# Decoder trunk: weights packed by the host into contiguous groups, x and p also passed transposed, and the first FFN chunk computed with weights stationary

## The chip, the cores and the metric

The kernel runs on one core of one Trainium2 chip. The metric is the device time of one execution in microseconds, the median over runs; lower is better. All inputs and the output are float32 in HBM. Whatever the host does to the inputs before the launch is not in the time.

## The reference, cut to what matters

```python
# x: (1, 256, 1024); p: (2, 1, 256, 256); DEPTH = 2, D_FF = 2816
def swiglu(x, w_in, w_out):
    h = x @ w_in                       # w_in: 1024 x 5632
    gate, up = h[..., :D_FF], h[..., D_FF:]
    return (silu(gate) * up) @ w_out   # w_out: 2816 x 1024

for i in range(DEPTH):
    if i == 1: k_nope, k_rope, v = shared_kv(x, ...)
    x = layer_norm(ALPHA * x + 0.5 * swiglu(x, ffn1_w_in[i], ffn1_w_out[i]))
    x = layer_norm(ALPHA * x + (fox_mixer(x) if i == 0 else mla_mixer(x)))
    x = layer_norm(ALPHA * x + 0.5 * swiglu(x, ffn2_w_in[i], ffn2_w_out[i]))
    gate = sigmoid(x @ ple_w_gate[i] + ple_b_gate[i])
    x = layer_norm(ALPHA * x + gate * (p[i] @ ple_w_proj[i]))
```

There are 256 tokens, two layers and four SwiGLU FFNs. The first layer mixes with forgetting attention (FoX), the second with multi-head latent attention (MLA).

## The kernel before, in words

**Precision.** Every operand of a matmul is split into a high part (rounded by an ACT copy into the float32r type) and a low part (source minus high part, by DVE). One product is three matmuls: high x high, high x low, low x high. The splits of weights are the lines `L194` (ACT) and `L195` (DVE) in the profile; the splits of activations are the helper `parts` (`L522` ACT, `L523` DVE). Nearly all matmuls are issued by the helper `mm`, line `L513`, and all transposes by `transpose`, `L517` (a matmul against the identity `ident`).

**Weights.** A class `Stream` owns the weights. A trial pass records in which order the program uses weight units; the real pass then loads groups of up to 128 x 2048 floats (1 MB) in that order into a ring of `NRAW = 3` raw buffers (`raw`). All loads are DMAs on SP's queue, and a raw buffer is loaded again once both of its units are split. Each unit (128 x 1024) is split into a slot: ten slots `hl`, and four tiles that are lent as slots while nobody else needs them (`ota`, `otb`, `qk`, `fs`). When a unit is split is decided while the program is built, from modelled times of PE, ACT, DVE and DMA; on the chip the order of each engine's instructions is then fixed. A weight in HBM lies as the reference has it, so a `w_in` group is read as two DMAs of 256-column strips, rows of 1 KB, and a `w_out` group as one DMA with rows of 4 KB.

**An FFN.** `ffn` walks over eleven chunks `c` of 256 gate and 256 up columns. `HT(c)` keeps a block of 128 weight columns stationary and streams the 256 tokens of the transposed activations `xT` (256 columns per matmul, 96 matmuls), so the hidden values come out transposed, as the second matmul needs them: SiLU and product (`L707`, `L708`), then `parts`. Chunks alternate between two rings of two PSUM banks, `h` and `tr`. `W(c)` multiplies with `w_out` into four `y` banks (512 columns per matmul). A chunk may be given a "turn", some transposes put between its first and second unit: `T(c)` transposes the hidden values of a chunk that came out with tokens on partitions, `ple_transpose` those of `p`, and `spare` transposes the identity.

**The very first chunk.** `first` computes chunk 0 of the first FFN (`cold=True`) while data still arrive. In `setup`, x is loaded in eight 128 x 256 pieces that alternate on SP's queue with pieces of the first weight groups, and two matmuls on the zeroed `mask` (`spin`, `L493`; the profile has two records for each) keep TensorE at work. `first` transposes x piece by piece (`turn`), spins twice more, and multiplies with x stationary and 512 weight columns moving (`part`, 48 matmuls), one 128-row slice `k` at a time, the two token tiles staggered. The hidden values have tokens on partitions and get SiLU and product per token tile (`act`, `L675`, `L676`); chunk 1 then carries the turn `T(0, "h")`. In all, sixteen transposes of x and four of chunk 0 run in this stage.

**The per-layer input p.** In the second FFN of each layer, `ple_load` loads p at chunk 6 and `ple_transpose` (four transposes and `parts`) is the turn of chunk 8.

**The rest.** FoX and MLA are orders written out by hand; LayerNorm is `ln` (its first read of x is `L574`, its scale and shift are loaded into `gb` by `load_gb`).

Of the kernel before, what the change touches and what calls it, by code (L numbers as in the profile page):

```python
# [31 lines left out]
FINE = 4  # L32
# [59 lines left out]
class Recorder:  # L92
# [10 lines left out]
    lend = reclaim = check = load = busy = pair = split = ahead = later = split_now = fill = pump  # L103
# [3 lines left out]
class Stream:  # L107
# [66 lines left out]
    def split(self, between=lambda: None, half=False):  # L174
# [18 lines left out]
        def part(c):  # L193
            nc.scalar.activation(hi[:, c], src[:, c], AF.Copy)  # L194
            nc.vector.tensor_tensor(lo[:, c], src[:, c], hi[:, c].bitcast(F32), op=ALU.subtract)  # L195

        if self.ready < FINE:
            self.hl[key] = w
            part(slice(0, 1))
            between()  # L200
            part(slice(1, 2))
        elif key[0] == "pb":
            nc.gpsimd.memset(w[:, 0, :].bitcast(F32), 0.0)
            lo = w[32:33, 0, :n]
            part(slice(None))
        elif half:
            nc.scalar.activation(hi, src, AF.Copy)
            self.busy(act=n)

            def rest():  # L210
                nc.vector.tensor_tensor(lo, src, hi.bitcast(F32), op=ALU.subtract)
                self.busy(dve=n)
                self.split_done(key, w)

            self.rest = rest
            return
        else:
            part(slice(None))
# [113 lines left out]
def make_loads(a):  # L332
    def rows(ap, k0, n):
        return ap[k0 * 128 : (k0 + n) * 128, :].rearrange("(k p) c -> p k c", p=128)

    def loads(q, g, raw, fine, between):
        k, i = g[0], g[-1]
        if k == "win":
            w = a[g[2]][0][g[1]]
            c = g[3]  # L340
            r = raw.rearrange("p (k c) -> p k c", c=512)
            n = fine
            for k0 in range(0, 4, n):
                if n == 1 and (i, k0) in between:
                    between[i, k0]()
                for s in range(2):
                    c0 = DFF * s + 256 * c
                    q.dma_start(
                        r[:, k0 : k0 + n, 256 * s : 256 * s + 256], rows(w[:, c0 : c0 + 256], 4 * i + k0, n)
                    )  # L350
        elif k == "fv":
            w = a["fox_w_in"][0]
            q.dma_start(raw.rearrange("p (k c) -> p k c", c=512), rows(w[:, 2048:2560], 4 * i, 4))
        elif k == "fvb":
            w = a["fox_w_in"][0]
            q.dma_start(raw.rearrange("p (k c) -> p k c", c=256), rows(w[:, 2560:2816], 0, 8))
        elif k == "fvc":
            w = a["fox_w_in"][0]
            n = 6 - 4 * i
            q.dma_start(raw[:, 0 : 272 * n].rearrange("p (k c) -> p k c", c=272), rows(w[:, 2816:3088], 6 * i, n))  # L360
        elif k in ("fk", "fq"):
            w = a["fox_w_in"][0]
            c = (1024 if k == "fk" else 0) + 256 * i
            q.dma_start(raw.rearrange("p (k c) -> p k c", c=256), rows(w[:, c : c + 256], 0, 8))
        elif k in ("wout", "fo", "pg", "pp", "mo"):
            if k == "wout":
                w = a[g[2]][1][g[1]]
            elif k == "fo":
                w = a["fox_w_o"][0]
            elif k == "mo":  # L370
                w = a["mla_w_o"][0]
            elif k == "pg":
                w = a["ple_w_gate"][g[1]]
            else:
                w = a["ple_w_proj"][g[1]]
            q.dma_start(raw.rearrange("p (k c) -> p k c", c=1024), rows(w, 2 * i, 2))
        elif k == "pb":
            q.dma_start(raw[0:1, 0:1024], a["ple_b_gate"][g[1] : g[1] + 1, :])
        elif k == "kd":
            q.dma_start(raw[:, 0:1280].rearrange("p (k c) -> p k c", c=320), rows(a["kv_w_down"], 4 * i, 4))  # L380
        elif k == "dq":
            q.dma_start(raw[:, 0:1536].rearrange("p (k c) -> p k c", c=384), rows(a["mla_w_dq"][0], 4 * i, 4))
        elif k == "qr":
            w = a["mla_w_uq"][0]
            for s in range(2):
                kk = 2 * i + s
                if kk < 3:
                    q.dma_start(
                        raw[:, 1024 * s : 1024 * s + 1024].rearrange("p (h d) -> p h d", d=64),
                        w[128 * kk : 128 * kk + 128, :, 128:192],  # L390
                    )
        elif k == "kvv":
            w = a["kv_w_up"]
            for kk in range(2):
                q.dma_start(
                    raw[:, 512 * kk : 512 * kk + 512].rearrange("p (h d) -> p h d", d=128),
                    w[128 * kk : 128 * kk + 128, 4 * i : 4 * i + 4, 128:256],
                )
        elif k == "kq":
            for kk in range(5):  # L400
                w, r = (a["kv_w_up"], kk) if kk < 2 else (a["mla_w_uq"][0], kk - 2)
                q.dma_start(
                    raw[:, 256 * kk : 256 * kk + 256].rearrange("p (h d) -> p h d", d=128),
                    w[128 * r : 128 * r + 128, 2 * i : 2 * i + 2, 0:128],
                )
        else:
            raise KeyError(g)
# [15 lines left out]
class Trunk:  # L423
# [33 lines left out]
    def setup(self):  # L457
# [29 lines left out]
        self.S.lend("ota", "otb", "qk", "fs")  # L487
# [12 lines left out]
    def load_x(self, t, q):  # L500
        c = slice(256 * q, 256 * q + 256)
        self.dma(self.x[t][:, c], None if self.rec else self.a["x"][0, 128 * t : 128 * t + 128, c])


# [100 lines left out]
    def ffn(self, li, which, lni, kv=False, ple=False, at=None, cold=False):  # L605
# [12 lines left out]
        def first():  # L618

            ps = [self.bank("h") for _ in range(2)]  # L620

            def part(t, k, w):
                for i, j in SWEEPS[4][0]:
                    self.mm(
                        ps[t], self.xT[:, t, i, k, :], w[:, j, 512 * (k % 2) : 512 * (k % 2) + 512],
                        k == 0 and (i, j) == (0, 0), k == 7 and (i, j) == SWEEPS[4][0][-1],
                    )

            def turn(t, q):
                tr = self.bank("tr")  # L630
                c = slice(2 * q, 2 * q + 2)
                for i in range(2):
                    k = 2 * q + i
                    self.transpose(tr[:, 128 * i : 128 * i + 128], self.x[t][:, 128 * k : 128 * k + 128])
                self.parts(
                    self.xT[:, t, 0, c, :], self.xT[:, t, 1, c, :],
                    tr[:, 0:256].rearrange("p (k c) -> p k c", c=128),
                )

            S.hold = True  # L640
            turn(0, 0)
            self.spin(2)
            old = None
            for u in range(4):
                key = ("win", li, which, 0, u)

                def mid():
                    turn(1, u)
                    if u:
                        part(1, 2 * u - 1, old)  # L650
                    part(0, 2 * u, S.hl.get(key, Dummy()))

                S.split(mid)
                if self.rec:
                    mid()
                w = old = self.use(key)
                if u < 3:
                    turn(0, u + 1)
                else:
                    S.split()  # L660
                part(0, 2 * u + 1, w)
                if u == 3:
                    act(0, 0, ps[0])
                    S.split()
                part(1, 2 * u, w)
            S.split()
            part(1, 7, w)
            S.hold = False
            act(0, 1, ps[1])
# [21 lines left out]
        def HT(c, what=None):  # L691
            ring = "tr" if c % 2 == cold else "h"
            ps = [self.bank(ring) for _ in range(2)]
            for u in range(4):
                if u == 1 + (cold and c == 1) and what:
                    what()
                w = self.use(("win", li, which, c, u))
                for kk, b in ((kk, b) for kk in range(2) for b in range(4)):
# [6 lines left out]
                    )  # L705
            gt = self.tl([128, 768], F32, "P", 2)[:, 0:512]
# [35 lines left out]
        def spare(ring):  # L742
# [33 lines left out]
    def ple_load(self, li):  # L776
        self.ple_p = self.tl([128, 512], F32, "g4", 5)
        for t in range(2):
            self.dma(
                self.ple_p[:, 256 * t : 256 * t + 256],  # L780
                None if self.rec else self.a["p"][li, 0, 128 * t : 128 * t + 128, :],
            )

    def ple_transpose(self):
        nc = self.nc
        pt = self.ple_p
        tr = self.bank("h")
# [831 lines left out]
```

## Time and profile before

| what | us |
|---|---|
| median of 3 runs | 1083.85 (1083.05 to 1084.26) |
| profiled execution, first to last instruction (span) | 1080.8 |
| what lies around the span, against the median | 3.05 |
| PE busy | 1065.8 |
| PE weight loads busy | 971.2 |
| DVE busy | 718.8 |
| ACT busy | 543.3 |

No time of its own is recorded for the profiled execution beside its span, so the span is set against the median of the runs. The busy time of an engine is the time in which it has an instruction in flight; matmuls are pipelined, so PE's busy time contains short gaps. In the chain that ended last each piece is followed back from the end of the program to what released it. The DMA queue moved 197.43 MB, at a mean of 184 GB/s over the span with the instruction loads.

### The profile page before, as it was taken

Reading aid. Unit: us, or ns where it says so; the run is one execution under the profiler, and the core shown is the slowest. Engines: PE = TensorE matmul, PEld = TensorE weight load, DVE = VectorE, ACT = ScalarE, POOL = GpSimd, SP = SyncE. Lnnn points to the kernel's source line nnn. Section 1 sums busy time; section 2 is a strip of 40 time slices with the busy share of each in tenths; the row PEclk is TensorE's granted clock in tenths of the full one; section 3 lists DMA queues with packets and bytes.
Section 4 is the critical chain, followed back from the end, with each engine's and each line's share of the span. In section 5 each row is a group of like instructions: output and inputs, shape, how many; then the busy total and the mean of one; then the engine's idle time right before and its main releaser. Section 6 shows DMA issues by size and latency. Waiting matters only on the chain.

```text
span 1080.8 us, 17731 instructions
## 1 busy us (share of the span) xinstructions
PE 1065.8 (99%) x7210; PEld 971.2 (90%) x7210; DVE 718.8 (67%) x1042; ACT 543.3 (50%) x806; POOL 73.2 (7%) x104
## 2 busy tenths in 40 slices
PE   9999999999999999999999999999999999999996
PEld 7989999899879999998899999988899889898986
DVE  4665645888797545558966564388777886455566
ACT  4565433666646444444555443336576465444431
POOL 0000000222200000000320000012200000000000
PEclk9999999999999999999999999999999999999999
DMA  8787752653358756455588564343445568565502
GB/s 270 230 312 241 245 181 83 195 166 137 114 172 290 254 181 190 148 201 156 164 275 266 185 194 165 89 105 112 140 145 169 174 225 308 191 206 192 182 13 78
DMA packets 151428, 198.54 MB, mean 184 GB/s; under 512 B 11954, under 2 KB 130994, under 8 KB 151348
## 3 DMA queue, kind: packets, MB, share of 16 engines
q1 hardware_dynamic: 151348, 197.43, 55.8%
q8 instruction: 56, 0.92, 0.3%
q14 instruction: 24, 0.20, 0.1%
HBM read 196.35 MB, written 1.05 MB: 183 GB/s over the span
## 4 chain that ended last, share of the span: by engine, by line
PE 90%; DVE 6%; issue 2%; ACT 2%; POOL 1%; DVEq 0%; POOLq 0%; ACTq 0%
PE y L513 32%; PE h L513 32%; PE tr L513 23%; PE tr L517 2%; DVE hl L195 2%; DVE x L593 1%; ACT hl L194 1%; DVE st L575 0%; DVE x L574 0%; PE h L517 0%; DVE PT L523 0%; ACT P L1460 0%; PE tr L1100 0%; DVE g L833 0%; POOL rs L585 0%
## 5 line engine op out<-in xcount | busy, mean ns | idle before, releaser
L195 DVE TENSOR_TENSOR hl<-raw,hl 128x1024 fp32r<-128x1024 f32 (+3 forms) x276 | 321.4, 1183 | 152.0 <-ACT hl L194 150.4
L194 ACT ACTIVATE hl<-raw 128x1024 fp32r<-128x1024 f32 (+3 forms) x276 | 274.4, 1016 | 187.0 <-PE y L513 95.0
L513 PE MATMUL y<-hl,g 128*128 128x512 f32 x816 | 190.7, 390 | 0.0
L513 PEld LDWEIGHTS y<-hl,g 128*128 128x128 f32 x816 | 152.0, 188 | 30.7
L513 PE MATMUL tr<-xT,hl 128*128 128x256 f32 x1512 | 177.3, 277 | 0.0
L513 PEld LDWEIGHTS tr<-xT,hl 128*128 128x128 f32 x1512 | 174.6, 188 | 0.9 <-DVE hl L195 0.2
L513 PE MATMUL h<-xT,hl 128*128 128x256 f32 x1464 | 174.0, 278 | 0.1
L513 PEld LDWEIGHTS h<-xT,hl 128*128 128x128 f32 x1464 | 170.0, 188 | 1.5 <-DVE qk L523 0.3
L513 PE MATMUL h<-hl,xT 128*128 128x512 f32 (+2 forms) x348 | 80.9, 379 | 0.5 <-DVE xT L523 0.4
L513 PEld LDWEIGHTS h<-hl,xT 128*128 128x128 f32 x348 | 61.5, 188 | 13.0 <-DVE xT L523 0.9
L513 PE MATMUL y<-hl,xT 128*128 128x512 f32 (+3 forms) x360 | 65.4, 334 | 0.0
L513 PEld LDWEIGHTS y<-hl,xT 128*128 128x128 f32 x360 | 55.5, 188 | 6.3 <-ACT xT L522 0.4
L585 POOL TENSOR_TENSOR rs<-ve,mhalf 128x1 f32<-128x1 f32 x16 | 15.2, 952 | 601.2 <-DVE ve L584 601.2
L522 ACT ACTIVATE xT<-tr 128x512 fp32r<-128x512 f32 (+1 forms) x36 | 19.2, 550 | 57.1 <-PE tr L517 57.0
L513 PE MATMUL y<-hl,otb 128*128 128x512 f32 x168 | 43.4, 399 | 0.7 <-DVE hl L195 0.5
L523 DVE TENSOR_TENSOR g<-P,g 128x512 fp32r<-128x512 f32 x37 | 25.6, 692 | 25.8 <-ACT g L522 25.8
L522 ACT ACTIVATE g<-P 128x512 fp32r<-128x512 f32 x37 | 23.4, 632 | 32.2 <-DVE P L708 32.2
L513 PEld LDWEIGHTS y<-hl,otb 128*128 128x128 f32 x168 | 30.2, 188 | 7.2 <-DVE hl L195 0.8
L195 DVE TENSOR_TENSOR otb<-raw,otb 128x1024 fp32r<-128x1024 f32 (+1 forms) x20 | 24.1, 1202 | 16.8 <-ACT otb L194 16.8
L195 DVE TENSOR_TENSOR qk<-raw,qk 128x1024 fp32r<-128x1024 f32 (+1 forms) x21 | 25.7, 1222 | 10.8 <-ACT qk L194 10.8
L707 ACT ACTIVATE P<-tr 128x512 f32<-128x512 f32 x20 | 12.0, 598 | 40.2 <-PE tr L513 40.2
L708 DVE TENSOR_TENSOR P<-P,tr 128x512 f32<-128x512 f32 x20 | 13.8, 688 | 26.8 <-PE tr L513 15.1
(259 smaller groups left out, 1411.6 us busy)
## 6 DMA issues: line engine op xcount, KB each, us to landing
raw<-in_ffn_w_in_dram SPq DMA_DIRECT2D x170, 512.0 KB, 4.8
raw<-in_ffn_w_out_dram SPq DMA_DIRECT2D x44, 1024.0 KB, 5.0
raw<-in_fox_w_in_dram SPq DMA_DIRECT2D x11, 1024.0 KB, 5.4
raw<-in_ple_w_gate_dram SPq DMA_DIRECT2D x8, 1024.0 KB, 5.1
raw<-in_mla_w_o_dram SPq DMA_DIRECT2D x8, 1024.0 KB, 5.0
gb<-in_ln_g_dram SPq DMA_DIRECT2D x8, 512.0 KB, 6.4
gb<-in_ln_b_dram SPq DMA_DIRECT2D x8, 512.0 KB, 7.8
raw<-in_fox_w_o_dram SPq DMA_DIRECT2D x4, 1024.0 KB, 4.9
```

The source lines that it names most:

```text
L194: nc.scalar.activation(hi[:, c], src[:, c], AF.Copy)
L195: nc.vector.tensor_tensor(lo[:, c], src[:, c], hi[:, c].bitcast(F32), op=ALU.subtract)
L513: self.nc.tensor.matmul(out, lhsT, rhs, start=start, stop=stop)
L517: self.nc.tensor.transpose(out, in_, self.ident)
L522: self.nc.scalar.activation(hi, src, AF.Copy)
L523: self.nc.vector.tensor_tensor(lo, src, hi.bitcast(F32), op=ALU.subtract)
L585: nc.gpsimd.tensor_tensor(rs, ve, self.mhalf, op=ALU.pow)
L593: nc.vector.scalar_tensor_tensor(xs, xs, rs if i else mv[:, 0:1], self.gb[:, i, c0:c1], op0=ALU.mult if i else ALU.subtract, op1=ALU.add i ...
L707: nc.scalar.activation(gt, ps[0], AF.Silu)
L708: nc.vector.tensor_tensor(gt, gt, ps[1], op=ALU.mult)
```

## The change

The host passes other arrays, and the kernel reads them:

- `_packed` reorders each weight so that every raw group is one contiguous block of 128 rows (8 KB per row for a full group). A group is then one DMA, with exceptions below. The gate and up strips of a `w_in` group lie together.
- x is passed as it is and transposed (`xt`, 128 x 8 x 256); p is passed transposed only (`pt`).
- `first` transposes nothing. `xraw`, which uses the tile `fs`, receives x transposed in five pieces; `parts` splits it into `xT` per slice k. Chunk 0 is computed with weights stationary as in `HT`, but per slice first the four blocks' high x high, then high weight x low x, then low weight x high x. SiLU, product and split are those of `HT`, now the function `close`; the turn `T(0, "h")` of chunk 1 is gone, and so is the second pair of spins.
- The first slice of x transposed and the second half of the first weight slice are loaded on ACT's queue, all else on SP's. The high part of the first 256 weight columns is made by DVE (`split_pieces`, "hi"), the others by ACT. All four units of chunk 0 are split slice by slice before the first matmul is issued, three more units during the chunk. `fs` is lent as a slot only after chunk 0's splits are issued.
- x itself is loaded at chunk 3 (`load_x`), two DMAs of 512 KB.
- `ple_split` splits the loaded tile directly; the four transposes of p in each layer are gone.

The order of PE's instructions is otherwise the same as before; on ACT and DVE some weight splits of the first FFN stand up to two units earlier.

```diff
@@ setup
-        self.load_x(0, 0)
-        x = lambda t, q: lambda: self.load_x(t, q)
-        self.S.between = {
-            (0, 1): x(1, 0), (0, 2): x(0, 1), (0, 3): x(1, 1),
-            (1, 0): x(0, 2), (1, 1): x(1, 2), (1, 2): x(0, 3), (1, 3): x(1, 3),
-        }
+        self.xraw = self.tl([128, 8, 256], F32, "fs", 1)
+        self.load_xt(0, 1, nc.scalar)
+        x = lambda *k: lambda: self.load_xt(*k, nc.sync)
+        self.S.between = {(0, 0, "half"): nc.scalar, (0, 1): x(1, 2), (0, 2): x(2, 4), (1, 0): x(4, 6), (1, 2): x(6, 8)}
...
-        self.S.lend("ota", "otb", "qk", "fs")
+        self.S.lend("ota", "otb", "qk")
@@ make_loads
         if k == "win":
-            ...
-                for s in range(2):
-                    c0 = DFF * s + 256 * c
-                    q.dma_start(
-                        r[:, k0 : k0 + n, 256 * s : 256 * s + 256], rows(w[:, c0 : c0 + 256], 4 * i + k0, n)
-                    )
+            w = a[g[2]][0][g[1], g[3], i]
+            for k0 in range(0, 4, fine):
+                between.pop((i, k0), lambda: None)()
+                c = slice(512 * k0, 512 * (k0 + fine))
+                half = between.pop((i, k0, "half"), None)
+                if half:
+                    m = 512 * k0 + 256
+                    q.dma_start(raw[:, c.start : m], w[:, c.start : m])
+                    half.dma_start(raw[:, m : c.stop], w[:, m : c.stop])
+                else:
+                    q.dma_start(raw[:, c], w[:, c])
@@ ffn.first
-            def part(t, k, w):
-                for i, j in SWEEPS[4][0]:
-                    self.mm(
-                        ps[t], self.xT[:, t, i, k, :], w[:, j, 512 * (k % 2) : 512 * (k % 2) + 512],
-                        ...
-            def turn(t, q):
-                ...
-                    self.transpose(tr[:, 128 * i : 128 * i + 128], self.x[t][:, 128 * k : 128 * k + 128])
-            turn(0, 0)
-            self.spin(2)
...
+            for u in range(4):
+                if u == 0:
+                    head = (("hi", 0, 0, 256), xs(0), ("lo", 0, 0, 256), ("both", 0, 256, 512))
+                else:
+                    head = (xs(2 * u), ("both", 0, 0, 512))
+                S.split_pieces(key(u), head + (xs(2 * u + 1), ("both", 1, 0, 512)))
+            S.lend("fs")
+            for u in range(4):
+                w = self.use(key(u))
+                for kk in range(2):
+                    k = 2 * u + kk
+                    for i, j in ((0, 0), (1, 0), (0, 1)):
+                        for b in range(4):
+                            self.mm(
+                                ps[b // 2][:, 256 * (b % 2) : 256 * (b % 2) + 256],
+                                w[:, j, 512 * kk + 128 * b : 512 * kk + 128 * b + 128], self.xT[:, :, i, k, :],
+                                (k, i, j, b % 2) == (0, 0, 0, 0), (k, j, b % 2) == (7, 1, 1),
+                            )
+                if u:
+                    S.split()
             S.hold = False
-            act(0, 1, ps[1])
+            close(0, ps)
@@ ffn
         turns = (
-            lambda: T(0, "h"),
+            None if cold else lambda: T(0, "h"),
             lambda: spare("h") if cold else T(1, "tr"),
-            self.kv_transpose if kv else self.ple_transpose if ple else lambda: spare("tr" if cold else "h"),
+            self.kv_transpose if kv else self.ple_split if ple else lambda: spare("tr" if cold else "h"),
         )
@@ ple
-    def ple_transpose(self):
-        ...
-            self.transpose(tr[:, c], pt[:, c])
+    def ple_split(self):
         self.ple_pT = self.tl([128, 2, 512], F32R, "g4", 5)
-        self.parts(self.ple_pT[:, 0, :], self.ple_pT[:, 1, :], tr)
+        self.parts(self.ple_pT[:, 0, :], self.ple_pT[:, 1, :], self.ple_p)
@@ run
-        self.ffn(0, "ffn1", 0, at={8: [keep("qk", "fs")]}, cold=True)
+        self.ffn(0, "ffn1", 0, at={3: [self.load_x], 8: [keep("qk", "fs")]}, cold=True)
@@ _packed (host), one line of it
+        w = a[n + "_w_in"].reshape(2, 2, 4, 128, 2, NCH, 256)
+        o[n + "_in"] = w.transpose(0, 5, 1, 3, 2, 4, 6).reshape(2, NCH, 2, 128, 2048)
```

More of the change, by code (lines that the diff above doesn't have):

```diff
@@ L101, in pump @@
         pass
-    lend = reclaim = check = load = busy = pair = split = ahead = later = split_now = fill = pump
+    lend = reclaim = check = load = busy = pair = split = split_pieces = ahead = later = split_now = fill = pump
     between, hl, hold = {}, {}, False
@@ L172, in later, with split @@
             f()
-    def split(self, between=lambda: None, half=False):
+    def split(self, half=False):
         self.later()
@@ L217, in split, with split_pieces @@
         else:
-            part(slice(None))
+            both()
+        self.pair(n)
+        self.split_done(key, w)
+    def split_pieces(self, key, todo):
+        nc = self.nc
+        assert key == self.order[self.ready]
+        src, _, n = unit_of(key, self.raw[group_of(key)])
+        slot = self.slots.pop(0)
+        self.slot_of[key] = slot
+        w = self.pool.tile([128, 2, 1024], F32R, tag=slot, name=slot, bufs=1)
+        hi, lo = (w[:, i, :].rearrange("p (a b) -> p a b", b=512) for i in range(2))
+        for x in todo:
+            if callable(x):
+                x()
+                continue
+            what, k, c = x[0], x[1], slice(*x[2:])
+            if what == "both":
+                nc.scalar.activation(hi[:, k, c], src[:, k, c], AF.Copy)
+            if what == "hi":
+                nc.vector.tensor_copy(hi[:, k, c], src[:, k, c])
+            else:
+                nc.vector.tensor_tensor(lo[:, k, c], src[:, k, c], hi[:, k, c].bitcast(F32), op=ALU.subtract)
         self.pair(n)
```

193 lines of the change are left out of this document (71 added, 122 removed).

## The prediction

> **What bounds the kernel now.** The page comes first, then the chain that ended last.
>
> ```profile
> span 1080.8 us, 17731 instructions
> PE 1065.8 (99%) x7210; PEld 971.2 (90%) x7210; DVE 718.8 (67%) x1042; ACT 543.3 (50%) x806; POOL 73.2 (7%) x104
> PE 90%; DVE 6%; issue 2%; ACT 2%; POOL 1%; DVEq 0%; POOLq 0%; ACTq 0%
> ```
>
> TensorE has something in flight 99% of the span and carries 90% of the chain. So a change pays where it takes instructions off PE or lets PE begin sooner, and hardly elsewhere. The timeline of the first 32 us shows how PE begins.
>
> ```profile
> 0.73 1.28 ACT L478 ACT_TABLE_LOAD   x1 [0.73 <-PEq L1605]
> 0.74 0.40 SPq L445 DMA_DIRECT2D x<-in_x_dram  x1
> 1.19 0.90 SPq L348 DMA_DIRECT2D raw<-in_ffn_w_in_dram  x2
> 1.20 2.93 PE L493 MATMUL y<-mask 128*128 128x384 f32 x4 [1.20 <-POOL mhalf L477]
> 3.29 0.23 PEld L517 LDWEIGHTS tr<-ident,x 128*128 128x128 f32 x1 [0.30 <-issue]
> 3.92 0.63 PE L517 MATMUL tr<-ident,x 128*128 128x128 f32 x2
> 4.80 1.65 PE L493 MATMUL y<-mask 128*128 128x384 f32 x4 [0.24 <-POOL mask L482]
> 6.42 0.93 PE L513 MATMUL h<-hl,xT 128*128 128x512 f32 x3
> 6.70 0.39 ACT L522 ACTIVATE xT<-tr 128x256 fp32r<-128x256 f32 x1 [1.20 <-PE tr L517]
> 6.98 0.62 ACT L194 ACTIVATE hl<-raw 128x512 fp32r<-128x512 f32 x1
> 7.12 0.42 DVE L523 TENSOR_TENSOR xT<-tr,xT 128x256 fp32r<-128x256 f32 x1 [0.90 <-ACT xT L522]
> 7.64 0.69 DVE L195 TENSOR_TENSOR hl<-raw,hl 128x512 fp32r<-128x512 f32 x1
> 17.69 1.06 ACT L194 ACTIVATE hl<-raw 128x1024 fp32r<-128x1024 f32 x1 [0.54 <-DMA raw<-in_ffn_w_in_dram]
> 18.78 1.23 DVE L195 TENSOR_TENSOR hl<-raw,hl 128x1024 fp32r<-128x1024 f32 x1 [0.90 <-ACT hl L194]
> 19.64 5.91 PE L513 MATMUL tr<-xT,hl 128*128 128x256 f32 x48
> 31.50 5.60 PE L513 MATMUL h<-xT,hl 128*128 128x256 f32 x48
> ```
>
> The columns are start, length, engine, line, operation and count. The first useful matmul starts at 6.42, chunk 0 lasts until 19.64, and chunk 1 until chunk 2 starts at 31.50. These pieces of the chain price PE's work:
>
> ```profile
> 12.78 0.22 PE tr L517 x2
> 13.00 1.37 PE h L513 x6
> 25.55 0.44 PE h L517 x4
> 42.54 10.88 PE tr L513 x96
> 64.30 27.21 PE y L513 x120
> 441.02 2.83 PE tr L513 x24
> 452.46 10.88 PE h L513 x96
> 993.10 2.83 PE tr L513 x24
> 1004.54 10.88 PE h L513 x96
> ```
>
> A 256-wide matmul costs 10.88 / 96 = 0.113 us, a 512-wide one 27.21 / 120 = 0.227 us, a transpose 0.11 us. From 31.50 until the first LayerNorm, PE is never late.
>
> **Part 1, matmuls of chunk 0.** Before: 48 matmuls of 512 columns with x stationary, 48 x 0.227 = 10.88 us. After: 96 of 256 columns with weights stationary, 96 x 0.113 = 10.88 us. The swap itself costs nothing. What it removes is transposing: chunk 0 comes out transposed already, so the turn T(0) inside chunk 1 goes (four transposes, 0.44 us; a chunk with a turn is priced below at 0.56 more), and with x passed transposed its sixteen transposes go, seven pairs of them after 6.42: 7 x 0.22 = 1.54 us.
>
> **Part 2, the start.** The second pair of spins (the four records at 4.80) goes, and the first matmul needs no transpose. It needs the first x^T slice, its high part from ACT, and the high part of the first 256 weight columns, now made by DVE at the same time. Both pieces are 128 KB, issued first on SP and on ACT. In before the first 128 KB, issued at 0.74, had landed by 3.29, where the weight load that needs x runs. Then 0.39 us on ACT gives 3.7; the first pair of spins (the four records at 1.20) holds PE until 3.92 whatever comes. I take 4.0. On ACT two issues of 0.45 us (two took 0.90 on SP) now stand ahead of the table load, which then runs from 1.6 to 2.9: covered, as ACT has no data before 3.3.
>
> The Trainium skill, "DMA: Bandwidth & Descriptors", section "Issuing engines are not separate DMA queues", speaks against the two-queue start: transfers from either engine share the same DMA engines, and only issue time is saved. By that the two first pieces come together about 0.4 us later than one alone (my estimate, 131 KB at the 351 GB/s of the rows below), the first matmul starts at 4.2 to 4.4, and the gain of the sum shrinks by 0.3 us; no run here shows a second queue yet.
>
> The four records of spinning at 1.20 took 2.93 us, the same four at 4.80 took 1.65: TensorE runs at about half speed until some 4.9. So 0.9 us of chunk 0 is done at half speed, 0.45 us lost.
>
> **Part 3, can the splits and loads keep up?** Per slice k of 128 rows, ACT needs 0.39 + 0.62 = 1.01 us, DVE 0.42 + 0.69 = 1.11 us, PE 12 x 0.113 = 1.36 us: PE stays the slowest. The loads by the windows:
>
> ```profile
> 0.00:5.00 5.00, 3.56 (x7) 1.84 (x8) 0.00 (x0) 1.89 (x4) 1.78 (x11) 1.00 0.54 165
> 5.00:10.00 5.00, 4.91 (x21) 3.23 (x22) 3.17 (x6) 2.47 (x6) 0.00 (x0) 1.00 0.81 246
> 10.00:15.00 5.00, 5.00 (x27) 4.05 (x26) 3.35 (x6) 2.91 (x8) 0.00 (x0) 1.00 0.89 252
> 20.00:25.00 5.00, 4.98 (x44) 4.95 (x44) 3.02 (x5) 1.41 (x3) 0.00 (x0) 1.00 1.06 351
> ```
>
> The last column is GB/s. Per k, SP issues three pieces (393 KB) in 3 x 0.475 = 1.43 us, at most 275 GB/s: the 250 of 5 to 15 us is a limit of issuing, since later, with larger issues, the same 1 KB rows reach 351. After, twelve issues on SP and two on ACT replace 24 on SP, so chunk 0's data is all issued by 6.5. I take 351. Then 0.83 MB is there at 5.0 (165 x 5) and all 3.15 MB at 5.0 + 2.32 / 0.351 = 11.6, a slice every 1.1 us, less than PE's 1.36. Chunk 0 ends at 4.0 + 0.45 + 10.88 = 15.3. Chunk 1's first half group (0.52 MB) lands at 13.1, and 1.06 on ACT and 1.23 on DVE make it usable at 15.4. Its second half is usable at 16.9 (needed 18.1); the next MB lands at 17.6 and its halves are usable at 19.9 and about 23.0, behind chunk 0's SiLU on ACT (needed 20.8 and 23.6). On ACT the split of that MB is queued ahead of the SiLU; only chunk 2, at 26, waits for the banks that SiLU frees. I allow 0.2 us: chunk 2 starts at 15.3 + 0.2 + 10.88 = 26.4, against 31.50, **5.1 us** sooner. By the parts removed: 2.4 (start) + 1.54 + 0.8 (stalls in chunk 0: 13.22 - 10.88 - 1.54) + 0.56 + 0.42 (stalls in chunk 1) - 0.45 - 0.2 = 5.1.
>
> **Part 4, p passed transposed.** A chunk with a turn lasts 452.46 - 441.02 = 11.44 us and 1004.54 - 993.10 = 11.44 us, one without 10.88. Both turns of p go; the split stays on ACT and DVE, reading the loaded tile. 2 x 0.56 = **1.1 us**.
>
> **Part 5, at nothing.** x itself is loaded later, 1.05 MB (3 us at 351) in SP's queue behind the first w_out load:
>
> ```profile
> 47.38 4.91 SPq L376 DMA_DIRECT2D raw<-in_ffn_w_out_dram  x3
> L574 DVE SCALAR_TENSOR_TENSOR x<-x,y x4: 669/675/686, 181.8 to 194.9; 128x512 f32<-128x512 f32 x4
> ACT hl L194 <- DMA raw<-in_ffn_w_in_dram: 16.4, 12, 2.8
> PE h L513 <- DVE hl L195: 1.6, 2, 1.0
> PE y L513 <- DVE hl L195: 0.5, 1, 0.5
> ```
>
> x is first read at 181.8. The later w_out loads and gb stand behind it on SP; w_out, issued from 47.38, is first multiplied at 64.30, so 3 us of delay are covered (without that cover they would be the cost). The packing of all other weights makes loads land sooner and saves SP issues. But ACT's 16.4 us of waiting for w_in is not PE's: PE waits 2.1 us in all for splits of weights, so 0 to 2.1 us could be won; I take 0, as those stalls stand in the MLA layer behind ACT and DVE work. A second DMA queue could lengthen what lies around the span; the nearest row, SP's first issue at 0.74, bounds that to 0.7, and I take 0.
>
> **Sum.** 5.1 + 1.1 = 6.2 us off the profiled span: 1080.8 - 6.2 = 1074.6. The median of the runs is 1083.85, 3.05 over the span; with that 1077.6.
>
> **The rivals.**
> *Supply keeps 252 GB/s* (the rate is the transfers' own and not issuing's). For: two rows show it. Against: 351 with the same row size. Chunk 0's data is then there at 14.2, chunk 1's last half group is usable at about 27.9, chunk 2 starts near 30.6: 0.9 + 1.1 = 2.0 us gained, 1081.8.
> *The clock comes late.* In before, spins fill PE up to 6.4 almost without a gap. After, the second pair is gone and PE may wait for slices. If full speed were granted a further stretch of 4.9 - 1.2 = 3.7 us later, half of it is lost: 1.85 us, gain 4.3, 1079.5. For: the half speed at 1.20. Against: the spins that precede 4.9 are kept. The Trainium skill, "TensorE: Matmul & The Clock Gate", part 1, has the mechanism: full clock is released after one busy window of about 3.4 us whose phase is free. That agrees with 2.93 against 1.65; whether a short gap at 4 us spoils the window no run here shows.
> *Packing pays elsewhere too:* the 2.1 us of split waits go as well, 1075.5.
> *Slower: 8 KB rows land later.* Per chunk of an FFN, 3 MB are loaded while PE works 10.88 + 24 x 0.227 us, so 1 MB per 5.44 us, in 132 groups over four FFNs. From 5.49 us per MB on (0.05 x 132 = 6.6) the gain is gone; at 5.55 the time is 1077.6 + 14.5 = 1092.1. For: long rows put more into one partition at a time, and nothing in the trace has 8 KB rows. Against:
>
> ```profile
> raw<-in_ffn_w_in_dram SPq DMA_DIRECT2D x170, 512.0 KB, 4.8
> raw<-in_ffn_w_out_dram SPq DMA_DIRECT2D x44, 1024.0 KB, 5.0
> ```
>
> w_out, with 4 KB rows, lands 1 MB in 5.0 us where w_in with 1 KB rows takes 4.8 for half of that, and up to three such groups overlap.
>
> **How the numbers follow.** Forecast 0.62; 252 GB/s 0.12; late clock 0.10; gain elsewhere 0.10; slower 0.06. What a measurement can tell here is about 0.2%, 2.2 us. The forecast, the late clock and the gain elsewhere are all faster by more; the 252 GB/s case lies on the edge, so 0.05 of it counts as faster: 0.87. Its other 0.07 is the same, 0.06 slower. The range runs from the gain elsewhere (1075.4 with the runs' spread) past the late clock to the supply case less 0.6 us (1081.2); it leaves out the slower case and most of the supply case.
>
> **What the profile after would show.** One pair of spins and then h matmuls of 128x256 from 4.0; no transposes before 26; chunk 1's tr matmuls from about 15.4 and chunk 2's h matmuls from about 26.4; 96 matmuls in one piece of 10.88 where p's turns were; 350 GB/s or more from 5 to 15 us. Wrong would be: chunk 1 starting after 17 (supply or clock, told apart by whether the h matmuls stand 0.113 or 0.21 us apart), chunk 2 at 26.4 but a gain under 4 us (given back later, most likely where DVE and POOL work together in MLA), or PE waits for splits in the FFNs.

## The result, and the profile after

The change made the kernel slower: 1090.36 us, median of 4 runs (1089.45 to 1091.73), against 1084.05 (1083.05 to 1084.57) for the kernel before in the same series. The ratio is 1.0056, 95% interval 1.0044 to 1.0068. The profiled execution took 1091.73 with a span of 1089.4. It was the slowest of the four. The page after:

```profile
span 1089.4 us, 17513 instructions
PE 1072.9 (98%) x7226; PEld 980.9 (90%) x7226; DVE 719.1 (66%) x1043; ACT 543.4 (50%) x805; POOL 73.2 (7%) x104
PE 89%; DVE 6%; ACT 2%; issue 1%; POOL 1%; DMA 0%; DVEq 0%; POOLq 0%; ACTq 0%
```

PE is busy for 7 us more although it has no more work: 48 matmuls of 512 columns became 96 of 256, and 28 transposes and four records of spinning are gone. The timeline of after, at the places that the prediction named:

```profile
0.73 0.41 ACTq L474 DMA_DIRECT2D fs<-in_xt_dram  x1
0.74 0.39 SPq L360 DMA_DIRECT2D raw<-in_ffn_in_dram  x1
1.21 2.93 PE L465 MATMUL y<-mask 128*128 128x384 f32 x4 [1.21 <-POOL mhalf L449]
5.42 0.29 DVE L233 CAST hl<-raw 128x256 fp32r<-128x256 f32 x1 [5.42 <-DMA raw<-in_ffn_in_dram]
5.58 0.42 ACT L497 ACTIVATE xT<-fs 128x256 fp32r<-128x256 f32 x1 [2.42 <-DMA fs<-in_xt_dram]
6.05 13.77 PE L488 MATMUL h<-xT,hl 128*128 128x256 f32 x96 [1.92 <-ACT xT L497]
30.96 5.82 PE L488 MATMUL h<-xT,hl 128*128 128x256 f32 x48
42.27 2.99 PE L488 MATMUL tr<-xT,qk 128*128 128x256 f32 x24
45.10 3.04 PE L488 MATMUL tr<-xT,fs 128*128 128x256 f32 x24
47.97 5.82 PE L488 MATMUL tr<-xT,hl 128*128 128x256 f32 x48
```

The first useful matmul starts at 6.05, chunk 0 takes 13.6 us, and chunk 2 starts at 30.96 (before: 31.50; forecast: 26.4). And the matmuls of `HT` themselves are slower: 48 last 5.82 where before they lasted 5.60. The same rows of the kernel before, which tell the slots apart:

```profile
42.38 2.88 PE L513 MATMUL tr<-xT,qk 128*128 128x256 f32 x24
45.10 2.88 PE L513 MATMUL tr<-xT,fs 128*128 128x256 f32 x24
47.82 5.60 PE L513 MATMUL tr<-xT,hl 128*128 128x256 f32 x48
```

Of 24 matmuls the row shows 23 steps and one whole matmul of 0.28: 2.88 is a step of 113 ns, 2.99 of 118, 3.04 of 120. So there are three paces. On `fs` the matmuls of after stand 120 ns apart, and those behind them 118. Counted over all steps between two matmuls of the form of `HT` in the trace, those at 115 ns or less fall from 3466 to 1675, those of 116 to 119 rise from 380 to 2069, those at 120 or 121 from 6 to 198; the time above 113.3 ns per step rises from 2.05 to 10.81 us. These 8.8 us are about the whole difference of the spans, 8.6. What else there is about cancels: three turns less, and in this one execution a short drop of the granted clock (the share of its full clock that PE was given) in MLA, 0.79 in the third column from the last, which made the stretch around it 0.9 us longer (columns: stretch, busy time of PE, its weight loads, DVE, ACT and POOL, granted clock, DMA share, GB/s):

```profile
762.00:770.00 8.00, 6.68 (x29) 5.53 (x30) 6.71 (x15) 3.74 (x9) 4.64 (x3) 0.79 0.54 204
```

Not all of the 8.8 us need hang on one cause. The 291 steps from 11 to 45 us stand at 118 here although no matmul reads `fs` as weights before 45.10; that is some 1.3 us. And in the third FFN, which does not use `fs`, nothing is lost: matched matmul by matmul, after is 4.65 us behind before at its start and 4.66 at its end.

The chain after shows the same at the places where the two turns of p were:

```profile
444.85 11.31 PE tr L488 x96
456.15 11.36 PE h L488 x96
1000.71 11.31 PE tr L488 x96
```

Forecast was 10.88 for each of them. Loads are no cause: PE's waits for splits of weights are the same to a tenth (1.6 and 0.5 us, L488 <- L194), and w_in's group, now one DMA of 1 MB, lands as fast as w_out's did:

```profile
raw<-in_ffn_in_dram SPq DMA_DIRECT2D x85, 1024.0 KB, 5.0
```

The first question was therefore what sets the three paces. One thing in the build differs that the diff does not say: `fs` is now the first of the weight slots to be allocated, and lies at byte 44704 of each partition, 32 modulo 128. It lay at 177888, 96 modulo 128, as all the other slots do in both kernels. `xT`, the moving operand (the one that streams past the weights), lies at 27296, 32 modulo 128.

### The profile page after: what moved, and what is told of

It reads as the page before. It is cut to its first block, busy times and chain, and to the rows that moved or that the text cites. A ratio compares the mean times of both kernels' runs of the same rounds, so it can differ in the third digit from the quotient of the medians.

```text
span 1089.4 us, 17513 instructions
## 1 busy us (share of the span) xinstructions
PE 1072.9 (98%) x7226; PEld 980.9 (90%) x7226; DVE 719.1 (66%) x1043; ACT 543.4 (50%) x805; POOL 73.2 (7%) x104
## 4 chain that ended last, share of the span: by engine, by line
PE 89%; DVE 6%; ACT 2%; issue 1%; POOL 1%; DMA 0%; DVEq 0%; POOLq 0%; ACTq 0%
PE h L488 32%; PE y L488 32%; PE tr L488 22%; DVE hl L194 2%; PE tr L492 2%; DVE x L568 1%; ACT hl L193 1%; DMA fs<-in_xt_dram 0%; DVE st L550 0%; DVE x L549 0%; ACT P L1413 0%; DVE PT L498 0%; PE tr L1053 0%; DVE g L786 0%; POOL rs L560 0%
## 5 line engine op out<-in xcount | busy, mean ns | idle before, releaser
L194 DVE TENSOR_TENSOR hl<-raw,hl 128x1024 fp32r<-128x1024 f32 (+3 forms) x268 | 315.9, 1198 | 154.5 <-ACT hl L193 153.6
L193 ACT ACTIVATE hl<-raw 128x1024 fp32r<-128x1024 f32 (+3 forms) x268 | 269.5, 1028 | 190.0 <-PE y L488 96.6
L488 PE MATMUL h<-xT,hl 128*128 128x256 f32 x1560 | 190.1, 281 | 2.2 <-ACT xT L497 1.9
L488 PE MATMUL y<-hl,g 128*128 128x512 f32 x816 | 190.9, 390 | 0.0
L488 PEld LDWEIGHTS h<-xT,hl 128*128 128x128 f32 x1560 | 185.6, 190 | 5.0 <-ACT xT L497 3.1
L488 PEld LDWEIGHTS y<-hl,g 128*128 128x128 f32 x816 | 152.0, 188 | 31.0
L488 PE MATMUL tr<-xT,hl 128*128 128x256 f32 x1512 | 179.8, 279 | 0.0
L488 PEld LDWEIGHTS tr<-xT,hl 128*128 128x128 f32 x1512 | 177.7, 189 | 0.5
L488 PE MATMUL h<-hl,xT 128*128 128x512 f32 (+2 forms) x300 | 67.8, 374 | 0.3 <-DVE xT L498 0.3
L488 PE MATMUL y<-hl,xT 128*128 128x512 f32 (+3 forms) x360 | 65.4, 334 | 0.0
L488 PEld LDWEIGHTS h<-hl,xT 128*128 128x128 f32 x300 | 53.2, 188 | 10.7 <-DVE xT L498 0.9
L488 PEld LDWEIGHTS y<-hl,xT 128*128 128x128 f32 x360 | 55.5, 188 | 6.4 <-ACT xT L497 0.4
L488 PE MATMUL y<-hl,otb 128*128 128x512 f32 x168 | 44.5, 407 | 0.7 <-DVE hl L194 0.5
L497 ACT ACTIVATE xT<-tr 128x512 fp32r<-128x512 f32 x28 | 16.1, 597 | 49.4 <-PE tr L492 49.4
L488 PEld LDWEIGHTS y<-hl,otb 128*128 128x128 f32 x168 | 31.0, 193 | 7.2 <-DVE hl L194 0.8
L194 DVE TENSOR_TENSOR otb<-raw,otb 128x1024 fp32r<-128x1024 f32 (+1 forms) x20 | 24.1, 1203 | 17.6 <-ACT otb L193 17.6
L194 DVE TENSOR_TENSOR qk<-raw,qk 128x1024 fp32r<-128x1024 f32 (+1 forms) x21 | 25.7, 1222 | 12.2 <-ACT qk L193 12.2
```

The lines of the kernel that those rows point to most:

```text
L488: self.nc.tensor.matmul(out, lhsT, rhs, start=start, stop=stop)
L497: self.nc.scalar.activation(hi, src, AF.Copy)
```

## The experiments

Each was timed beside runs of the kernel before on its chip; ratios are to that kernel.

### fs 64 bytes further

```diff
+        self.tl([128, 1], F32, "ss", 2)
         self.xraw = self.tl([128, 8, 256], F32, "fs", 1)
```

> The changed kernel with the small tile ss allocated ahead of fs, so that the weight slot fs starts 64 bytes higher in each partition (44768 instead of 44704) and every other tile stays where it was; no instruction differs. Theory PACE (the loss is a slower pace of the 256-wide matmuls, 0.118 to 0.120 us instead of 0.113, which the place of fs sets off and which lasts until a turn of transposes): the matmuls that read fs return from 0.120 to 0.113 or 0.118, no chunk falls into the slow pace at fs, and the time drops by 4 to 5 us, to about 1085.5 to 1086. Theory LOADS (rows of 8 KB land late or disturb the engines): no change, 1090. Theory START (all is lost in the first 30 us): no change, 1090.

1083.77 us, ratio 1.000 (0.9991 to 1.001). 64 bytes win 6 us, more than expected. The rows at the same place:

```profile
41.80 2.88 PE L489 MATMUL tr<-xT,qk 128*128 128x256 f32 x24
44.52 2.88 PE L489 MATMUL tr<-xT,fs 128*128 128x256 f32 x24
47.24 5.60 PE L489 MATMUL tr<-xT,hl 128*128 128x256 f32 x48
```

The pace of 120 is gone, and with it the slow matmuls behind it. 4.37 us above 113.3 ns are left, 2.6 of them in chunks 8 to 10 of the two second FFNs. The rest of the change is then worth nothing: chunk 2 starts at 30.92.

### The turns put back as spare ones

```diff
-            None if cold else lambda: T(0, "h"),
+            lambda: spare("h") if cold else T(0, "h"),
     def ple_split(self):
+        tr = self.bank("h")
+        for k in range(4):
+            self.transpose(tr[:, 128 * k : 128 * k + 128], self.ident)
```

> The changed kernel with four transposes of the identity put back where each of the three turns was removed (chunk 1 of the first FFN, chunk 8 of both second FFNs); their results are not used. Theory PACE: although twelve transposes are added, the 256-wide matmuls after each turn return to 0.113 us until fs is read; 0.5 to 2 us faster than the changed kernel, 1088.4 to 1089.9. The prediction's pricing of a turn (0.56 us each, nothing else): 1.1 to 1.7 us slower, 1091.5 to 1092. Theories LOADS and START: like that pricing.

1088.12 us, ratio 1.0037 (1.0024 to 1.0049): 2 us less than after, for twelve transposes more. The trace gives the turns only a part of it: the first FFN stands at 113 from the start of the clock on, already ahead of its turn, which is worth the 1.3 us named above.

Both edits so far together, fs moved and the turns back:

> Both edits together: fs 64 bytes higher and the three turns put back. Theory PACE: nearly all 256-wide matmuls after the first 25 us at 0.113, 7 us faster than the changed kernel, about 1083.4. The prediction's pricing of turns: no better than the first edit alone plus 1.1 us. Theories LOADS and START: 1091 or more.

1081.72 us, ratio 0.9979 (0.9971 to 0.9988). In the profiled execution part of it is the start: here the clock came at 4.7 and chunk 0 took 10.95 us for 94 matmuls. The chunks 8 to 10 take 33.2 us again. But behind the turn in chunk 1 the matmuls stay at 118 (one chunk 11.31), so a turn does not always help.

### The first pieces on one queue

```diff
-        self.load_xt(0, 1, nc.scalar)
+        self.load_xt(0, 1, nc.sync)
-        self.S.between = {(0, 0, "half"): nc.scalar, ...
+        self.S.between = {(0, 0, "half"): nc.sync, ...
```

> The changed kernel with the two loads that stood on ACT's queue (first slice of x transposed, second half of the first weight slice) moved to SP's queue; all loads are on one queue. Theory START (two queues at once make the first pieces land late: 5.4 to 5.6 us instead of 2.9 to 3.5): the first h matmul starts at 4 to 4.5 instead of 6.05, and with no long pause the clock is released at about 5 instead of 10.6; 2 to 4 us faster, 1086.5 to 1088.5. Theories PACE and LOADS: within 1 us of the changed kernel, unless the first pieces are what they name.

1087.0 us, ratio 1.0027 (1.0018 to 1.0036). The first pieces arrive 2 us sooner and the first matmul starts at 4.08, as forecast, but then the second slice is missing:

```profile
3.09 0.42 ACT L497 ACTIVATE xT<-fs 128x256 fp32r<-128x256 f32 x1 [0.86 <-DMA fs<-in_xt_dram]
3.64 0.29 DVE L233 CAST hl<-raw 128x256 fp32r<-128x256 f32 x1 [3.64 <-DMA raw<-in_ffn_in_dram]
4.08 2.24 PE L488 MATMUL h<-xT,hl 128*128 128x256 f32 x12
7.58 0.63 ACT L231 ACTIVATE hl<-raw 128x512 fp32r<-128x512 f32 x1 [2.18 <-DMA raw<-in_ffn_in_dram]
8.26 3.92 PE L488 MATMUL h<-xT,hl 128*128 128x256 f32 x18 [1.94 <-ACT hl L231]
```

The granted clock falls behind that gap: in the windows of this run 9 to 12 us read

```profile
9.00:12.00 3.00, 3.00 (x17) 3.00 (x16) 2.74 (x6) 2.77 (x7) 0.00 (x0) 0.54 1.06 393
```

(third column from the last: 0.54 of full clock). Chunk 1 starts at 19.5, no sooner than in after. So in this trace the earlier arrival wins nothing; the gap and the clock behind it take the same time. That the run as a whole is 3 us faster than after, as the theory of the start expected, is therefore not shown to come from the start. In this trace it comes from the pace: 113 instead of 118 up to `fs`, and 8.43 us above 113.3 ns in all against 10.81. And this execution, of 1089.33 us, is the slowest of the run's eleven, 2.3 us over the median; how the start went in the others no trace shows.

### Packing alone, in the kernel before

`_packed` and the loads of after in the kernel before; x, p, chunk 0 and the pieces' order as before.

```diff
-                for s in range(2):
-                    c0 = DFF * s + 256 * c
-                    q.dma_start(r[:, k0 : k0 + n, 256 * s : 256 * s + 256], rows(w[:, c0 : c0 + 256], 4 * i + k0, n))
+                c = slice(512 * k0, 512 * (k0 + fine))
+                q.dma_start(raw[:, c], w[:, c])
```

> The kernel before with the packing of the weights alone (one transfer of 1 KB or longer rows per group in place of two; x and p as before, chunk 0 as before). Packing at nothing (the prediction's part 5, and the trace of after, in which PE's waits for splits are the same 1.6 and 0.5 us): 1083.7, within 1 us. Packing does harm (longer rows, other arrivals): up to 3 us slower. Packing pays: fewer issues at the start bring chunk 2 forward from 31.50, 1 to 2 us faster.

1083.87 us, ratio 0.9994 (0.9986 to 1.0003): nothing, as forecast.

### The place of fs alone, in the kernel before

```diff
         nc.gpsimd.memset(self.mask, 0.0)
+        self.tl([128, 8, 256], F32, "fs", 1)
```

> The kernel before with the slot fs allocated right after rope, as in the kernel after (byte 44704 of a partition, 32 modulo 128, where all other weight slots have 96); nothing else of the change. Theory slot (a weight tile at that offset makes its matmuls stand 120 ns apart and leaves those behind it at 117.8): about 4 to 5 us slower than before, 1088 to 1089, with matmuls 120 ns apart on fs. Rival (the slower pace comes from the missing turns or the new start, the offset only goes with it): 1083.7, no matmuls at 120.

1090.52 us, ratio 1.0062 (1.0048 to 1.0075). That is 2 us more than expected: one allocation moved, no instruction changed, and the kernel before is as slow as the kernel after. The groups of matmuls and weight loads on `fs`, of the kernel before and of this one:

```profile
L513 PEld LDWEIGHTS tr<-xT,fs 128*128 128x128 f32 x72 | 8.4, 188 | 0.0
L513 PE MATMUL tr<-xT,fs 128*128 128x256 f32 x72 | 8.6, 276 | 0.0
```

```profile
L514 PEld LDWEIGHTS tr<-xT,fs 128*128 128x128 f32 x72 | 8.8, 192 | 0.0
L514 PE MATMUL tr<-xT,fs 128*128 128x256 f32 x72 | 9.1, 283 | 0.0
```

A weight load from `fs` takes 192 ns instead of 188, a matmul 7 ns more. That is only about 1.4 us on the 206 steps that the trace has there; most of the loss is the 118 ns that the other slots' matmuls keep after `fs`, until the next W stage (the matmuls of `W`): 8.59 us above 113.3 ns here against 2.05.

### What the place must be relative to

```diff
+        self.tl([128, 16], F32, "pad", 1)
         self.xT = one([128, 2, 2, 8, 128], F32R, "xT")
```

> After with 64 unused bytes ahead of xT, so that xT, fs and all weight slots lie 64 bytes further: xT and fs now at 96 modulo 128, the other slots at 32. If what counts is how a weight tile lies to xT, the moving operand (same offset modulo 128: slow): fs alone stays at 120 ns, the time is that of after, 1089 to 1091. If what counts is the weight tile's own offset (32: slow): fs is fast and all other slots are at 120 ns, some 5500 matmuls by 5 to 7 ns: 1110 to 1125. If neither: all at 113.3, 1084.

1088.07 us, ratio 1.0032 (1.0021 to 1.0042). `xT` and `fs` are now at 96, the others at 32, and it is still `fs` alone:

```profile
39.90 2.88 PE L489 MATMUL tr<-xT,qk 128*128 128x256 f32 x24
42.62 3.04 PE L489 MATMUL tr<-xT,fs 128*128 128x256 f32 x24
```

So it is not the weight tile's own offset. The time is 2 us below after, a little better than expected. In the profiled execution the clock came at 8.9 and chunk 2 started at 29.0, which would do it; how the other six started no trace shows. The other distances, with the padding of 32 bytes put behind `xT`, so that `fs` lies 32 and the rest 96 bytes from `xT`'s offset:

```diff
+        self.tl([128, 8], F32, "pad", 1)
         self.xraw = self.tl([128, 8, 256], F32, "fs", 1)
```

> After with 32 unused bytes between rope and fs: fs lies 32 bytes from xT's offset modulo 128, the other weight slots 96 (in after 0 and 64). If only the same offset as xT's is slow: no matmuls 120 ns apart, the time of after with fs moved by 64, about 1084. If 32 and 96 are slow too (only 64 is good): 120 ns on fs and on the other slots, 1110 or more; if 32 alone: 1089 to 1091.

1100.33 us, ratio 1.0156 (1.0141 to 1.0171):

```profile
43.94 3.01 PE L489 MATMUL tr<-xT,qk 128*128 128x256 f32 x24
46.79 2.99 PE L489 MATMUL tr<-xT,fs 128*128 128x256 f32 x24
49.62 5.86 PE L489 MATMUL tr<-xT,hl 128*128 128x256 f32 x48
```

Now nothing is at 113; 118 to 119 ns is the mean on every slot. Less than the 1110 expected, since the steps vary from 115 to 122 and don't stand at 120. For these matmuls, of four distances between the weights' and the moving operand's offsets modulo 128, 64 is good, 0 the worst (120), 32 and 96 lie between. That the period is 128 bytes is not shown: within their tiles both operands start in steps of 512 bytes, so the runs can't tell 128 from 256 or 512.

### Four spins, fs moved, p's turns put back

```diff
+        self.tl([128, 1], F32, "ss", 2)
         self.xraw = self.tl([128, 8, 256], F32, "fs", 1)
-        self.spin(2)
+        self.spin(4)
     def ple_split(self):
+        tr = self.bank("h")
+        for k in range(4):
+            self.transpose(tr[:, 128 * k : 128 * k + 128], self.ident)
```

> After with fs 64 bytes further, the two turns of p put back as spare ones, and four spins at the start in place of two. Theory: the first matmul comes at about 6.3 on a TensorE already at full clock (released at about 5), chunk 0 ends at 17.2 to 17.5, chunk 2 starts at 28.3 to 29, chunks 8 to 10 of both second FFNs run at 113.3 ns: 1079 to 1080.5, 1 to 2.5 us below the kernel with the turns and fs moved. Rival (the late start of the clock is not set by the gap before the first matmul, or supply holds chunk 0 anyway): chunk 2 at 30 or later, 1081 to 1082.5.

1080.78 us, ratio 0.9967 (0.9954 to 0.9979): faster than both kernels. The windows from 7 to 10 us, first of after, then of this kernel, count PE's matmuls in the first brackets:

```profile
7.00:10.00 3.00, 3.00 (x15) 3.00 (x16) 2.69 (x7) 2.72 (x7) 0.00 (x0) 1.00 0.94 343
```

```profile
7.00:10.00 3.00, 3.00 (x29) 3.00 (x28) 2.75 (x7) 2.36 (x6) 1.09 (x3) 1.00 0.98 337
```

Fifteen against twenty-nine: half speed in after. (The clock column reads 1.00 there too: the trace has no clock record yet. The first grants of full clock are recorded at 10.6 and 6.6.) Chunk 2 starts at 28.99. What the two spins alone are worth is less certain. Over two queues, with two spins, chunk 2 started at 30.92, 30.96, 29.0 and 32.6 in the traces without the turn in chunk 1, and the run with both edits, two spins and one turn more, reached 0.9979 (0.9971 to 0.9988), which overlaps with this one. With the first pieces on one queue as well (the diff of the one-queue run):

> The kernel with fs moved, p's turns put back and four spins, and the first x and weight pieces issued on SP instead of ACT. Theory: the first pieces are there by about 3.6, so the first matmul follows the spins at 6.0 to 6.3 at full clock, as with two queues; the second slice of weights, there at 7.6 to 8.3 in the one-queue run, is needed at 7.5: chunk 2 starts within 0.7 us of the two-queue kernel's 28.99, 1080.5 to 1081.5. Rival (the split over two queues is what holds the start back even with the spins): chunk 2 at 27.5 to 28.3, 1079.5.

1081.25 us, ratio 0.9974 (0.9965 to 0.9983), the same within the intervals. Its chain begins

```profile
6.69 11.11 PE h L489 x96
17.81 10.88 PE tr L489 x96
28.69 10.88 PE h L489 x96
```

With the clock up, chunk 0 takes little more than its 10.88 here; in the run above, over two queues, it took 11.5 from its first matmul to chunk 1's.

### What a turn does to the pace

```diff
-                HT(c, turns[i] if c == group[0] else None)
+                HT(c, (lambda: spare("tr")) if cold and c == 2 else turns[i] if c == group[0] else None)
```

> The kernel with fs moved, p's turns put back and four spins, and a spare turn (four transposes of the identity) inside chunk 2. Theory (a turn sets the 256-wide matmuls back to 113.3 ns): the 300 matmuls from chunk 2 to the first W stage, which stood 117.8 apart, stand 113.3 apart behind it: 1.3 won, 0.56 paid, W stage about 0.7 us earlier. Rival (what sets the pace is something else): they stay at 117.8, 0.5 us lost.

```profile
29.28 2.99 PE L489 MATMUL h<-xT,hl 128*128 128x256 f32 x24
32.11 0.60 PE L493 MATMUL tr<-ident 128*128 128x128 f32 x4
32.46 2.98 PE L489 MATMUL h<-xT,hl 128*128 128x256 f32 x24
35.28 2.88 PE L489 MATMUL h<-xT,ota 128*128 128x256 f32 x24
```

118 before the turn, 113 behind it, up to the W stage, which starts 0.7 us nearer to chunk 2 than without the turn, as expected. It is not the only way to that pace: the one-queue run with four spins, without this turn, stood at 113 from chunk 0 on. In the total it can't be told: 1081.26, ratio 0.998 (0.997 to 0.999). And the prediction's part 4 by itself, in the kernel before:

```diff
-        self.kv_transpose if kv else self.ple_transpose if ple else ...
+        self.kv_transpose if kv else self.ple_split if ple else ...
```

> The kernel before with p passed transposed and its two turns taken out, nothing else. The prediction's part 4: a turn costs 0.56, chunk 8 shrinks from 11.44 to 10.88 in both second FFNs, 1.1 us faster. Theory pace (the turn is what ends the slower pace that follows a W stage): chunks 8 to 10 last 33.9 in place of 33.2 in each, 1.4 us slower in all.

1084.98 us, ratio 1.0012 (1.0002 to 1.0021): slower, by 0.2 to 2.3 us. Its chain:

```profile
441.58 11.31 PE tr L513 x96
452.89 11.31 PE h L513 x96
464.19 11.31 PE tr L513 x96
994.46 11.31 PE tr L513 x96
```

Three chunks at 11.31 make 33.93 us where one with a turn and two without made 11.44 + 2 x 10.88 = 33.20; twice, 1.46 us lost.

## Why the prediction was wrong, point by point

**A term that was missing: where `fs` lies.** The prediction costed instructions and transfers and held 0.113 us per matmul fixed. The new order of allocation alone costs 5.2 to 8.1 us (1.0062, in the kernel before), as much as the whole result. It could not be read from the diff; that `fs` lies elsewhere could be read from the built program's addresses, but no trace had shown that this matters. The rival that ended slower (long rows landing late, 1092.1) came near the time by luck: its mechanism is another, one that the packed kernel before excludes.

**Part 1, the swap.** Right where the clock was up: chunk 0's 96 matmuls took 11.11 in the one-queue run with four spins. What it said of T(0) goes the way of part 4.

**Part 2, the start: the step that failed first.** First pieces at 3.29 and the first matmul at 4.0 were forecast; they came at 5.4 and 5.6, and at 6.05. The Trainium skill, "DMA: Bandwidth & Descriptors", section "Issuing engines are not separate DMA queues", says that a second issuing engine saves only issue time. In this case it brought PE nothing sooner, and the estimate drawn from it, 0.4 us later, was too small: with both queues the pieces were usable 2 us later than with one. Then the clock: half speed was allowed until 4.9, 0.45 us. PE stood idle from 4.1 to 6.05, full clock came at 10.6, and chunk 0 took 13.61 instead of 11.33: 2.28 us more. The prediction's own sign for this showed: chunk 1 started after 17, at 19.66, and until the clock came the h matmuls stood 0.21 us apart. The rival "the clock comes late" had named this at 1.85 us, with a chance of 0.10; its argument against (the first spins are kept) held only as long as the first matmul followed them at 4.0, and it came 1.9 us behind their end. With two more spins, which close the gap, chunk 2 started at 28.99 instead of 30.92, in one trace each. The Trainium skill's rule on the clock ("TensorE: Matmul & The Clock Gate", part 1: one busy window of some 3.4 us, of free phase) fits: full clock came 4.5 us behind the first matmul in after, 3.8 us behind the first spin in before (at 5.0), 5.4 and 5.8 behind it with four spins; in all fourteen traces it is 3.3 to 6.4 us behind the start of the stretch of work that led to it. So the same start can cost some us more or less from one execution to the next, and the 2.28 us are one execution's. The free phase shows in the run with both edits above, where the clock came at 4.7 although it too had a gap of 1.3 us.

Of the 5.1 us, 4.6 were lost so: 2.05 by the first matmul, 2.28 by chunk 0, 0.2 by the pace of chunk 1.

**Part 3, supply.** Half right. The rate was 343 GB/s from 5 to 10 us and 294 from 10 to 15, where 351 was forecast, so the rival of 252 GB/s is out. But chunk 0's data was not there at 11.6. SP, which issued these loads without a wait in before, waited 2.1 us for the first slice of x to land before it issued the third load of x, at 5.57, and ACT stood waiting for the seventh slice of weights until 14.13:

```profile
14.13 0.63 ACT L231 ACTIVATE hl<-raw 128x512 fp32r<-128x512 f32 x1 [1.51 <-DMA raw<-in_ffn_in_dram]
```

At half speed PE did not need it sooner, so it cost nothing in after. The forecast's chunk 0, begun at 4.0, would have needed it at about 12.6 (4.0 + 0.45 + 6 x 1.36), so its end at 15.3 was out of reach. In the one-queue run a slice came too late already at the start: the second, at 7.58, 3 us behind the first.

**Part 4, p's turns.** Wrong in sign: 1.46 us lost for 1.1 won. The rows for it were on the page. A chunk with a turn was priced as a whole, 11.44; its pieces were, in the kernel before,

```profile
444.28 8.18 PE tr L513 x72
996.36 8.18 PE tr L513 x72
```

behind the 24 in 2.83 that the prediction quotes: 118 ns each ahead of the turn, 113.6 behind. So 0.1 of the turn's 0.56 was the slow pace ahead of it, and what it bought was the normal pace for the chunks after it.

**Part 5.** Right: packing is worth nothing, and the later load of x costs nothing: DVE's first read of x waits 4.3 us for PE in both traces, not for a load.

**The sum:** start 0.5 instead of 5.1 won, p's turns 1.5 lost instead of 1.1 won, `fs` 5.2 to 8.1 lost instead of nothing: 6.2 to 9.1 us slower. Measured: 4.8 to 7.4. The terms overlap, since chunks 8 to 10 pay for the slow pace only once.

## To carry to other kernels

Where PE runs without a gap, the step between two matmuls is the first number to watch: take it from rows before and after, per tile, before looking for waits. When an edit allocates a tile earlier, compare the addresses of all matmul operands, and if two builds differ by a few nanoseconds per matmul, move one tile by 64 bytes, as here. And before removing work that looks idle (spins, spare transposes), read the pace and the clock of the matmuls behind it: here the turns of 0.56 that p no longer needed were worth more than they cost, and two more spins in idle time came with a start up to 2 us sooner.

## What the hardware did that was not expected

- The step of 256-column fp32r matmuls, each with its own weights, depends on the place of the weights relative to the moving operand: 113.3 ns at a distance of 64 bytes modulo 128, 120 at 0, 118 to 119 on the mean at 32 and 96. It is not the same for every form. In the W stage the slot is the moving operand and the hidden values are stationary: those 512-column matmuls stood 227 ns apart where both had the same offset, and 233 on `fs` in after, where they lay 64 apart.
- The same matmuls at the good distance have a second pace, 117.8 ns, that lasts for hundreds of matmuls. A W stage usually leaves it behind, matmuls on a badly placed tile did so in every FFN that uses `fs`, and four transposes ended it in nearly all places. In three traces (after, the turns put back, the place of `fs` alone) the turn at 945 to 947 us began it instead. What decides between the two paces is open; no run here looked further.
- Why the first pieces came later over two queues is open too, but the traces narrow it. A load reports its landing in sixteen parts. Over two queues the first part of the two first pieces came at 2.8 to 3.1 in all eight traces and the last at 4.6 to 6.2; over one queue the last came at 3.1 to 3.6. So a few of the sixteen parts are late, not the whole piece. It mattered less when spins covered the time.
